# An mLSTM's gate chain in two parts, its selectors in a stage buffer, conditioning steps moved, and latent squares in two sums

## The chip, the cores and the metric

The kernel runs on one core of a Trainium2 chip. The core has five engines with queues of their own that work in order: TensorE (PE, matmuls into PSUM), VectorE (DVE), ScalarE (ACT), GpSimd (POOL) and SyncE (SP, which issues the transfers here). The metric is the device time of one launch in microseconds (us), the median of several runs.

## The reference, cut to what matters

Two layers over 512 latent and 256 context tokens of 1024 channels. Layer 0 mixes tokens with a bidirectional mLSTM, layer 1 with windowed attention; a squared-ReLU MLP follows each, and all are modulated by a conditioning vector.

```python
for i in range(DEPTH):                       # 2 layers
    mod_l = split(silu(c) @ ada_w[i] + ada_b[i], 6);  mod_c = the same with c_ctx
    u = modulate(rms_norm(h, norm_mix[i]), mod_l[0], mod_l[1])       # latent
    uc = modulate(rms_norm(hc, norm_mix[i]), mod_c[0], mod_c[1])     # context
    y, yc = mixer(uc, u)
    h = h + mod_l[2] * y
    h = h + mod_l[5] * sq_relu_mlp(modulate(rms_norm(h, norm_ffn[i]), mod_l[3], mod_l[4]), w1, w2)
    ...                                      # the same for hc
return rms_norm(h, final_norm)

# the mLSTM, per head and direction, in chunks of 128 tokens
q, k, v, o, gates = split(u @ w_in, splits)      # log_i, log_f = gate, log_sigmoid(gate)
b = cumsum(log_f)
m = running maximum of the stabiliser;  w = exp(...), exp(-m)
h = (wq @ v + carry_w * (q @ c0)) / maximum(abs(den), exp(-m))
y = (rms_norm(h) * head_norm * sigmoid(o)) @ w_out
```

## The kernel before

All products are of fp32 data. Each factor is split into a high part and a rest (`whi` and `wlo` of a weight, `uH` and `uL` of the latent activations), and `mm3` (L96 to L98) makes three matmuls of them. Weights come in units of 128 x 1024: SP transfers one to a slot of `raw` (a ring of three slots in this stage), ACT casts it to `whi` (L876), and DVE, or POOL where the caller says so, makes `wlo` (L877). `whi` and `wlo` have four slots each. PSUM is used by two rings, `mm` with three banks and `at` with five. The tokens are treated in two groups, C (256 context columns) and L (512 latent ones).

The conditioning product that isn't needed at the start is spread through the program in steps: `ada_step` (from L249) transfers 512 KB to a slot of the same `raw` ring and multiplies it on DVE in one or two instructions (`adap`, L261). Who calls it decides where they lie: the output gate (`ogate`, by `dense_steps`) at each unit taken, `v_steps` at every second row block, `ada_until` at the MLP's first part.

Layer 0's mixer is `layer0_mix`. It projects q, k and the gates, starts the generator `gates`, runs `v_steps` for the first heads' v (v copied out of PSUM by ACT at L698), then the output gate of the first head pair (`ogate(0)`, copied out at L715), then the rest of the gates, and then `core(p)` for four head pairs p, between whose steps the projections of the next pair are put. `gates` makes a chain of some twenty small instructions on 40 partitions by 768 columns: log-sigmoid on ACT (L613, L614), running sums and maxima as scans on DVE (L619 to L623), three exponentials on ACT (L646, L651, L652), rests on POOL (L625, L642, L648), and then transposes on PE whose results ACT copies to `tok1` and `tok2` (L659, L664). `core` begins with transposes of k (L750), the products `kp` on DVE (L753) and `carry` (L740), a matmul of the gate rows `cst` with the selectors `es`, which POOL writes in `new_es` (L721).

Between the mixer and the MLP, the output projection of the latents (`out_late`) adds to hL; for each of its eight blocks ACT squares the new hL (L290) and the squares are added up into one tile `ssL` (L294), five adds on POOL and then two on DVE. `norm_rc` (L307) sums that over partitions on PE, DVE and POOL make the reciprocal root (L310, L312), and PE spreads it (L320). The MLP's first part, `plain` in `ffn0`, works beside this: four hidden blocks m, first for C (needing no latents), with two hooks after m=0 and m=1 that run the norm, then for L, then `back` multiplies the hidden blocks `h` with the second weight.

The order on each engine is set by a scheduler with a cost model of its own, which may move instructions against the order of the code; `keep_in_program_order` pins one. The line numbers are those of the kernel before; in the kernel after they are one higher in the first hundreds and up to eleven higher from `gates` on (L642 is L653 there, L646 L657, L648 L659, L651 L662, L652 L663, L698 is L709, L740 is L751, L753 is L764, L876 is L887, L877 is L888, L261 is L262).

## Time and profile before

| what | value |
|---|---|
| median of three runs | 1568.58 us (1566.23 to 1571.36) |
| the profiled execution | 1573.33 us, span 1571.5 us |
| PE busy | 1519.8 us, 97% of the span |
| DVE busy | 1123.5 us, 71% |
| ACT busy | 744.2 us, 47% |
| POOL busy | 341.3 us, 22% |

PE has 52 us without work, so most of what a reordering can give lies in its waits and in the stretches after them in which its granted clock is below full. The timeline rows below tell, for each instruction, when it started, how long it or the group took, and in brackets how long its engine had been idle before it and what ended that. SPq rows are the issues of transfers.

### The profile page before, as it was taken

The numbers are of one execution on the slowest core, as the hardware profiler recorded it, in microseconds if no ns is written. First come the engines' busy times: TensorE is split into PE (matmuls) and PEld (weight loads), VectorE is DVE, ScalarE is ACT, GpSimd is POOL, SyncE is SP. The second block draws the span as 40 slices with busy tenths as digits, with TensorE's granted clock in tenths as the row PEclk, the third lists the DMA queues.
The fourth block names the chain that finished last, engine by engine and source line by source line (L and its number), as shares of the span: only waits on it lengthen the run. The fifth ranks groups of instructions, "written<-read, shape, count | busy, mean of one in ns | idle before, by whom it ended". The sixth has DMA issues, their size and how long they took to land.

```text
span 1571.5 us, 23851 instructions
## 1 busy us (share of the span) xinstructions
PE 1519.8 (97%) x9110; PEld 1365.5 (87%) x9110; DVE 1123.5 (71%) x2064; ACT 744.2 (47%) x1506; POOL 341.3 (22%) x333
## 2 busy tenths in 40 slices
PE   7989999999999999999999999899999999999998
PEld 5778888878889999999999999788887888888886
DVE  3666556478777797876776668777888785767687
ACT  4534343334473533424325255566666665545454
POOL 0221111112213222233223322354443100000000
PEclk9989999999999999999999999999999999999999
DMA  8323223234321343343443421011101424150321
GB/s 311 131 74 108 94 95 94 79 101 138 101 68 67 105 136 123 133 148 119 149 135 120 134 81 66 23 41 41 41 28 55 157 82 151 40 170 32 107 68 54
DMA packets 47849, 157.28 MB, mean 100 GB/s; under 512 B 5327, under 2 KB 8911, under 8 KB 47607
## 3 DMA queue, kind: packets, MB, share of 16 engines
q1 hardware_dynamic: 46560, 154.25, 29.4%
q8 instruction: 72, 1.18, 0.3%
q10 hardware_dynamic: 1175, 1.51, 0.3%
q14 instruction: 42, 0.34, 0.1%
HBM read 153.64 MB, written 2.10 MB: 99 GB/s over the span
## 4 chain that ended last, share of the span: by engine, by line
PE 71%; DVE 8%; issue 6%; POOL 5%; ACT 4%; DMA 1%; POOLq 0%; DVEq 0%; ACTq 0%
PE mm L96 16%; PE mm L97 16%; PE mm L98 16%; DVE adap L261 2%; PE p L98 2%; PE p L96 2%; PE p L97 2%; PE pt L1793 1%; PE pj L96 1%; PE pj L98 1%; PE pj L97 1%; DVE wlo L877 1%; PE at L832 1%; ACT whi L876 1%; PE av L1809 1%
## 5 line engine op out<-in xcount | busy, mean ns | idle before, releaser
L877 DVE TENSOR_TENSOR wlo<-raw,whi 128x1024 fp32r<-128x1024 f32 (+2 forms) x152 | 182.6, 1205 | 87.9 <-ACT whi L876 87.1
L876 ACT CAST whi<-raw 128x1024 fp32r<-128x1024 f32 (+2 forms) x155 | 154.0, 1000 | 139.1 <-PE mm L97 74.7
L96 PE MATMUL mm<-uH,whi 128*128 128x512 f32 (+1 forms) x496 | 191.4, 390 | 3.9 <-ACT v L698 3.9
L97 PE MATMUL mm<-uL,whi 128*128 128x512 f32 (+1 forms) x496 | 188.8, 382 | 0.4 <-DVE uL L331 0.4
L98 PE MATMUL mm<-uH,wlo 128*128 128x512 f32 (+1 forms) x496 | 188.9, 382 | 0.0
L261 DVE SCALAR_TENSOR_TENSOR adap<-raw,crow 128x1024 bf16<-128x1024 f32 x128 | 167.0, 1305 | 21.6 <-DMA raw<-ada 20.8
L96 PE MATMUL mm<-h,whi 128*128 128x384 f32 x512 | 173.7, 339 | 4.0 <-DVE hL L1110 2.2
L97 PE MATMUL mm<-h,whi 128*128 128x384 f32 x512 | 172.9, 338 | 0.5 <-DVE h L877 0.5
L98 PE MATMUL mm<-h,wlo 128*128 128x384 f32 x512 | 172.6, 337 | 0.0
L96 PEld LDWEIGHTS mm<-uH,whi 128*128 128x128 f32 x496 | 94.0, 191 | 19.8 <-ACT v L698 4.2
L876 ACT CAST whi<-sum 128x512 fp32r<-128x512 f32 (+1 forms) x42 | 31.8, 760 | 166.3 <-PE mm L97 76.4
L98 PEld LDWEIGHTS mm<-uH,wlo 128*128 128x128 f32 x496 | 94.5, 191 | 17.9 <-issue 0.3
L97 PEld LDWEIGHTS mm<-uL,whi 128*128 128x128 f32 x496 | 94.6, 191 | 17.0 <-issue 1.0
L96 PEld LDWEIGHTS mm<-h,whi 128*128 128x128 f32 x512 | 96.4, 188 | 5.2 <-ACT h L876 2.6
L97 PEld LDWEIGHTS mm<-h,whi 128*128 128x128 f32 x512 | 96.4, 188 | 1.3 <-DVE h L877 1.2
L98 PEld LDWEIGHTS mm<-h,wlo 128*128 128x128 f32 x512 | 96.5, 188 | 0.0
L877 DVE TENSOR_TENSOR wlo<-wb,whi 128x1024 fp32r<-128x1024 f32 x49 | 59.2, 1222 | 35.9 <-ACT whi L876 35.8
L877 DVE TENSOR_TENSOR h<-r,h 128x384 fp32r<-128x384 f32 (+2 forms) x100 | 56.6, 568 | 35.4 <-ACT h L876 35.2
L876 ACT CAST whi<-wb 128x1024 fp32r<-128x1024 f32 x49 | 51.6, 1054 | 60.9 <-PE mm L97 27.1
L98 PE MATMUL p<-t,wlo 128*128 128x384 f32 x224 | 75.4, 337 | 0.3 <-DVE wlo L877 0.3
L97 PE MATMUL p<-t,whi 128*128 128x384 f32 x224 | 75.2, 336 | 0.0
L96 PE MATMUL p<-t,whi 128*128 128x384 f32 x224 | 75.2, 336 | 0.0
(396 smaller groups left out, 4175.2 us busy)
## 6 DMA issues: line engine op xcount, KB each, us to landing
raw<-ada SPq DMA_DIRECT2D x80, 512.0 KB, 3.5
raw<-w SPq DMA_DIRECT2D x64, 512.0 KB, 3.5
raw<-w2a SPq DMA_DIRECT2D x32, 512.0 KB, 3.5
wb<-w2b SPq DMA_DIRECT2D x28, 512.0 KB, 3.6
adaw<-ada SPq DMA_DIRECT2D x16, 512.0 KB, 5.7
hL<-xT SPq DMA_DIRECT2D x16, 256.0 KB, 3.7
raw<-wqk SPq DMA_DIRECT2D x8, 512.0 KB, 4.0
raw<-wv SPq DMA_DIRECT2D x8, 512.0 KB, 3.5
```

What stands on the lines that cost most here:

```text
L96: mm(out=out, lhsT=ah, rhs=bh, start=start, stop=False)
L97: mm(out=out, lhsT=ah, rhs=bl, start=False, stop=False)
L98: mm(out=out, lhsT=al, rhs=bh, start=False, stop=stop)
L261: self.tc.keep_in_program_order(nc.vector.scalar_tensor_tensor(out=pr, in0=w, scalar=0.5, in1=self.crow[:, v, :], op0=ALU.mult, op1=ALU.mu ...
L832: mm(out=o[hh][:, i * VW:(i + 1) * VW], lhsT=pw[g, d, hh][:, i, :], rhs=v[:, 3 * g + i, hh, :], start=False, stop=i == 2)
L876: keep(self.nc.scalar.copy(out=hi, in_=src))
L877: keep((eng or self.nc.vector).tensor_tensor(out=lo, in0=src, in1=hi.bitcast(F32), op=ALU.subtract))
L1793: nc.tensor.transpose(out=pt[:, i * P:(i + 1) * P], in_=ps_[i][:, n * P:(n + 1) * P], identity=self.ident)
L1809: mm(out=o, lhsT=vv, rhs=pl, start=False, stop=n == len(blks) - 1)
```

## The change

1. **Gate chain in two parts.** `gates` yields once more, behind the scans; `layer0_mix` runs it to there before the output gate is begun. The subtraction t1 = li - b (L625) moves from POOL to DVE. The three exponentials are pinned to each other's order.
2. **Selectors.** `es` comes from the pool of the stage (`ml`) instead of the mixer's (`mc`), and the first `new_es` is called before the output gate.
3. **Conditioning steps.** A `dense_steps` call that has POOL make `wlo` (the first output gate) calls no `ada_step`; `v_steps` of later pairs call it at three of six row blocks (j = 4, 5, 0) instead of at j = 1, 3, 5.
4. **Latent squares.** In layer 0's output projection the first four blocks' squares go into a sum L on POOL, the other four into a sum D on DVE, and one more add on DVE (L560 of the kernel after) joins them.
5. **First part of the MLP.** One unit of w1 fewer is fed ahead, the fourth is fed inside the C blocks; the hooks of the norm come after m=1 and in the middle of m=2; the L blocks run in pairs, the first four of their eight channel blocks interleaved, the rest one block after the other.

```diff
@@ -106,7 +106,8 @@
                     w[m] = self.unit(srcs(m), eng)
                 else:
                     w[m] = self.take(eng)
-                    self.ada_step()
+                    if not eng:
+                        self.ada_step()
             hi, lo = w[m]
             n = xs[g](0)[0].shape[-1]
             ps = self.mm.tile([P, 512], F32, name="mm", tag="mm")
@@ -286,7 +287,7 @@
         elif kt:
             sq = self.np.tile([P, n], F32, name="sq", tag=f"sq{n}", bufs=2)
         else:
-            sq = self.np.tile([P, n], F32, name=f"ss{g}", tag=f"ss{n}", bufs=1 if n == 512 else 2)
+            sq = self.np.tile([P, n], F32, name=f"ss{g}", tag=f"ss{n}", bufs=2)
         nc.scalar.activation(out=sq, in_=h, func=AF.Square)
         if apart or kt == 0:
             st.setdefault(g, []).append(sq)
@@ -297,15 +298,15 @@
 
         return self.norm_bc(self.norm_rc(st, g))
 
-    def norm_rc(self, st, g):
+    def norm_rc(self, st, g, keep=lambda i: i):
 
         nc = self.nc
         nb = st[g][0].shape[-1] // P
         ps = self.at.tile([P, 512], F32, name="at", tag="at")
         for j in range(nb):
             for i, acc in enumerate(st[g]):
-                nc.tensor.matmul(out=ps[:, j:j + 1], lhsT=acc[:, j * P:(j + 1) * P], rhs=self.ones, start=i == 0,
-                                 stop=i == len(st[g]) - 1)
+                keep(nc.tensor.matmul(out=ps[:, j:j + 1], lhsT=acc[:, j * P:(j + 1) * P], rhs=self.ones, start=i == 0,
+                                      stop=i == len(st[g]) - 1))
         rs = self.np.tile([P, 4], F32, name="rs", tag="rs", bufs=2)[:, 0:nb]
         nc.vector.tensor_scalar(out=rs, in0=ps[:, 0:nb], scalar1=1.0 / D, scalar2=EPS, op0=ALU.mult, op1=ALU.add)
         rc = self.np.tile([P, 4], F32, name="rc", tag="rc", bufs=2)[:, 0:nb]
@@ -439,10 +440,12 @@
             self.qk_out(qkv, (acc["C"][1:], acc["L"][1:]))
             for _ in self.v_steps(0, qkv[2], rows, wv):
                 pass
+            next(gt)
             self.begun, self.plan = [], [a["wo"][i] for i in range(2)]
             for p in range(1, 4):
                 self.plan += [a[w][2 * p + i] for w in ("wo", "wqk", "wv") for i in range(2)]
             self.plan += [a["wout"][m, :, 0:6 * P] for m in range(6)]
+            self.new_es(0)
             so = self.ogate(0, xs, nc.gpsimd)
             for _ in range(6):
                 next(so)
@@ -451,7 +454,6 @@
             with tc.tile_pool(name="mc", bufs=1, reuse_waits="tile") as mc:
                 self.mc = mc
                 self.late = []
-                self.new_es(0)
                 yu = {}
                 for p in range(4):
                     core = self.core(p, qkv)
@@ -548,7 +550,14 @@
                 for i in range(2):
                     sl = slice((m % 4 * 2 + i) * P, (m % 4 * 2 + i + 1) * P)
                     self.mm3(t, wl[m // 4][0][:, sl], wl[m // 4][1][:, sl], *xs[g](6 + i), new and i == 0, i == 1)
-                self.norm_add(self.st, g, n, self.out_add(m, g, t), nc.vector if n > 5 else None)
+                x = self.out_add(m, g, t)
+                if g == "C":
+                    self.norm_add(self.st, g, n, x, nc.vector if n > 5 else None)
+                else:
+                    self.norm_add(self.st, "DL"[n < 4], n % 4, x, nc.vector if n > 3 else None)
+                    if n == 7:
+                        s0, s1 = self.st["L"][0], self.st["D"][0]
+                        nc.vector.tensor_tensor(out=s0, in0=s0, in1=s1, op=ALU.add)
                 if g == "L" and n < 2:
                     hooks[n]()
             hooks = self.norm_hooks(g)
@@ -564,7 +573,7 @@
             else:
                 self.u0["L"] = self.new_u(cx=False)["L"]
             self.norm_whole(g, int(g == "C"), x[0])
-        return [lambda: x.append(self.norm_rc(st, g)), whole]
+        return [lambda: x.append(self.norm_rc(st, g, self.tc.keep_in_program_order)), whole]
 
     def gates(self, psc, psl):
 
@@ -622,7 +631,9 @@
             scan(m[FW, 0:NL], lf[FW, 0:NL], li[FW, 0:NL], m[FW, T - 1:T], op0=ALU.add, op1=ALU.max)
             scan(m[BW][:, ::-1], lf[BW][:, ::-1], li[BW][:, ::-1], 0.0, op0=ALU.add, op1=ALU.max)
             nc.vector.tensor_tensor(out=aa, in0=b, in1=m, op=ALU.subtract)
-            nc.gpsimd.tensor_tensor(out=t1[R], in0=li, in1=b, op=ALU.subtract)
+            nc.vector.tensor_tensor(out=t1[R], in0=li, in1=b, op=ALU.subtract)
+            yield
+            keep = tc.keep_in_program_order
 
             cp = nc.vector.tensor_copy
             cp(out=ae[FW], in_=aa[FW, P - 1::P])
@@ -643,13 +654,13 @@
 
             az = b
             nc.vector.tensor_tensor(out=ch(az), in0=ch(aa), in1=bc(m0), op=ALU.add)
-            nc.scalar.activation(out=az, in_=az, func=AF.Exp)
+            keep(nc.scalar.activation(out=az, in_=az, func=AF.Exp))
             cp(out=cst[R], in_=az)
             nc.gpsimd.tensor_tensor(out=cst[64:104], in0=az, in1=cst[R].bitcast(F32), op=ALU.subtract)
 
             nc.vector.tensor_tensor(out=ch(aa), in0=ch(t1[R]), in1=bc(ae), op=ALU.add)
-            nc.scalar.activation(out=t1[64:104], in_=aa, func=AF.Exp)
-            nc.scalar.activation(out=t2, in_=m, func=AF.Exp, scale=-1.0)
+            keep(nc.scalar.activation(out=t1[64:104], in_=aa, func=AF.Exp))
+            keep(nc.scalar.activation(out=t2, in_=m, func=AF.Exp, scale=-1.0))
             yield
             for c0, n in ((0, 4), (4, 2)):
                 ps = self.at.tile([P, 512], F32, name="at", tag="at")
@@ -696,7 +707,7 @@
                 if kt == 3:
                     yield
             self.nc.scalar.copy(out=v[:, j, :, 0:128], in_=ps[:, :256].rearrange("p (h e) -> p h e", e=128))
-            if p and j % 2:
+            if p and j in (4, 5, 0):
                 self.ada_step()
             yield
 
@@ -717,7 +728,7 @@
 
     def new_es(self, p):
 
-        self.es = self.mc.tile([104, 2, P], F32R, name="es", tag="es", bufs=2)
+        self.es = self.ml.tile([104, 2, P], F32R, name="es", tag="es", bufs=2)
         self.nc.gpsimd.tensor_copy(out=self.es.rearrange("r d (h e) -> r d h e", e=64),
                                    in_=self.esel.rearrange("r (d c) -> r d c", d=2)[:, :, 2 * p:2 * p + 2].unsqueeze(3)
                                    .broadcast_to([104, 2, 2, 64]))
@@ -1007,32 +1018,55 @@
 
         def plain(hid):
 
-            ws = [self.begun.pop(0) for _ in range(4)]
+            ws = self.begun
+            self.begun = []
             pools = [("mm", self.mm)] * 3 + [("at", self.at)]
-            for g in "CL":
-                xs = self.xs(self.u0)
-                for m in range(4):
-                    hi, lo = ws[m]
-                    n = xs[g](0)[0].shape[-1]
-                    ps = pools[m][1].tile([P, 512], F32, name="mm", tag=pools[m][0])[:, :n]
-                    for kt in range(KT):
+
+            def xs(g, kt):
+                return self.xs(self.u0)[g](kt)
+
+            def begin(g, m):
+                n = xs(g, 0)[0].shape[-1]
+                return pools[m][1].tile([P, 512], F32, name="mm", tag=pools[m][0])[:, :n]
+
+            def part(g, m, ps, half):
+                hi, lo = ws[m]
+                for kt in range(4 * half, 4 * half + 4):
+                    sl = slice(kt * P, (kt + 1) * P)
+                    self.mm3(ps, hi[:, sl], lo[:, sl], *xs(g, kt), kt == 0, kt == KT - 1)
+                if not half:
+                    return
+                r = r_tile(ps.shape[-1])
+                nc.scalar.activation(out=r, in_=ps, func=AF.Relu)
+                nc.scalar.activation(out=r, in_=r, func=AF.Square)
+                if g == "C":
+                    self.split(r, *[x[:, P:H] for x in hid[m][1]])
+                else:
+                    self.split(r[:, 0:H], *hid[m][0])
+                    self.split(r[:, H:NL], *[x[:, 0:P] for x in hid[m][1]])
+            for m in range(4):
+                ps = begin("C", m)
+                part("C", m, ps, 0)
+                if m == 2:
+                    hooks[1]()
+                part("C", m, ps, 1)
+                if m == 1:
+                    hooks[0]()
+                    self.feed(True)
+                    ws.append(self.begun.pop())
+            for i in range(2):
+                pss = [begin("L", 2 * i + m) for m in range(2)]
+                for kt in range(4):
+                    for m in range(2):
+                        hi, lo = ws[2 * i + m]
                         sl = slice(kt * P, (kt + 1) * P)
-                        self.mm3(ps, hi[:, sl], lo[:, sl], *xs[g](kt), kt == 0, kt == KT - 1)
-                    r = r_tile(n)
-                    nc.scalar.activation(out=r, in_=ps, func=AF.Relu)
-                    nc.scalar.activation(out=r, in_=r, func=AF.Square)
-                    if g == "C":
-                        self.split(r, *[x[:, P:H] for x in hid[m][1]])
-                        if m < 2:
-                            hooks[m]()
-                    else:
-                        self.split(r[:, 0:H], *hid[m][0])
-                        self.split(r[:, H:NL], *[x[:, 0:P] for x in hid[m][1]])
-                        self.feed()
-                        if m % 2:
-                            blocks(m // 2)
-                        if m == 1:
-                            self.ada_until(0, 5)
+                        self.mm3(pss[m], hi[:, sl], lo[:, sl], *xs("L", kt), kt == 0, False)
+                for m in range(2):
+                    part("L", 2 * i + m, pss[m], 1)
+                    self.feed()
+                blocks(i)
+                if i == 0:
+                    self.ada_until(0, 5)
 
         def seven(hid, m0, m1):
             banks = [("mm", self.mm), ("at", self.at)] * 3 + [("at", self.at)]
@@ -1117,8 +1151,7 @@
                 self.plan += [f for i in range(2) for f in pair_w1(4 * c + i, 4 * c + 2 + i)]
             self.plan += [unit_w2(c, i) for i in range(4)]
         self.plan += [lambda pr=pr, i=i: self.unit(a["wskv"][pr, i]) for pr in range(2) for i in range(2)]
-        for _ in range(2):
-            self.feed(True)
+        self.feed(True)
         for c in range(NC):
             hid = [[pair(f"h{t}", k) for t in range(2)] for k in range(4)]
             if c == 0:
```

**ACT, the copies of v, the exponentials and what follows before the mixer's heads.** In the names, `whi_999` and `whi_1172` are the third and fourth unit of the output gate's weight wo and `whi_1302` the first of wqk (`whi_993`, `whi_1160`, `whi_1290` after). Before:

```order
L698 COPY v_702<-mm_760 128x2x128
L652 ACT_TABLE_LOAD
L652 ACTIVATE gi_653<-m_655 40x768
L698 COPY v_702<-mm_786 128x2x128
L646 ACTIVATE b_656<-b_656 40x768
L698 COPY v_702<-mm_812 128x2x128
L651 ACTIVATE t1_658<-aa_657 40x768
L876 CAST whi_999<-raw_997 128x1024
L698 COPY v_702<-mm_838 128x2x128
L876 CAST whi_1172<-raw_1170 128x1024
L715 ACTIVATE hL0_907<-mm_882 128x512
```

After:

```order
L709 COPY v_687<-mm_745 128x2x128
L709 COPY v_687<-mm_771 128x2x128
L709 COPY v_687<-mm_797 128x2x128
L887 CAST whi_993<-raw_991 128x1024
L709 COPY v_687<-mm_823 128x2x128
L657 ACT_TABLE_LOAD
L657 ACTIVATE b_656<-b_656 40x768
L662 ACTIVATE t1_658<-aa_657 40x768
L663 ACTIVATE gi_653<-m_655 40x768
L887 CAST whi_1160<-raw_1158 128x1024
L726 ACTIVATE hL0_903<-mm_878 128x512
L887 CAST whi_1290<-raw_1288 128x1024
```

All copies of v and the cast of wo's third unit now stand ahead of the table load, which waits for DVE's L645, and exp(-m), which waited for the scan and stood among the copies, comes last of the three.

**POOL, the same place.** `wlo_1000` is the split of wo's third unit (`wlo_994` after). Before:

```order
L877 TENSOR_TENSOR wlo_867<-raw_864,whi_866 128x1024
L877 TENSOR_TENSOR wlo_873<-raw_870,whi_872 128x1024
L625 TENSOR_TENSOR t1_658<-gi_653,b_656 40x768
L642 TENSOR_TENSOR ast_644<-aa_657,ast_644 40x768
L648 TENSOR_TENSOR cst_645<-b_656,cst_645 40x768
L877 TENSOR_TENSOR wlo_1000<-raw_997,whi_999 128x1024
L721 COPY es_958<-esel_633 104x256
```

After:

```order
L682 MEMSET v_687 128x12
L732 COPY es_864<-esel_633 104x256
L682 MEMSET v_956 128x12
L732 COPY es_1278<-esel_633 104x256
L888 TENSOR_TENSOR wlo_869<-raw_866,whi_868 128x1024
L888 TENSOR_TENSOR wlo_875<-raw_872,whi_874 128x1024
L653 TENSOR_TENSOR ast_644<-aa_657,ast_644 40x768
L888 TENSOR_TENSOR wlo_994<-raw_991,whi_993 128x1024
```

The subtraction L625 is gone from POOL, the split of wo's third unit stands ahead of `cst`, and the first two selectors are written ahead of the splits.

**DVE, the head pair p=2, ahead of kp.** `wlo_2582` is a unit of wo, `wlo_2713` the first of the next wqk (`wlo_2700` after). Before:

```order
L261 SCALAR_TENSOR_TENSOR adap_2537,mod0_81<-raw_2535,crow_625 128x1024
L261 SCALAR_TENSOR_TENSOR adap_2539,mod0_81<-raw_2535,crow_625 128x1024
L877 TENSOR_TENSOR wlo_2582<-raw_2579,whi_2581 128x1024
L267 TENSOR_TENSOR mod0_81<-mod0_81,sm_67 128x16
L261 SCALAR_TENSOR_TENSOR adap_2587,mod0_81<-raw_2585,crow_625 128x1024
L261 SCALAR_TENSOR_TENSOR adap_2589,mod0_81<-raw_2585,crow_625 128x1024
L753 TENSOR_TENSOR kp_2550<-at_2551,tok1_646 128x384 x2
L753 TENSOR_TENSOR kp_2550<-at_2557,tok1_646 128x384 x2
```

After:

```order
L262 SCALAR_TENSOR_TENSOR adap_2447,mod0_81<-raw_2445,crow_625 128x1024
L262 SCALAR_TENSOR_TENSOR adap_2449,mod0_81<-raw_2445,crow_625 128x1024
L262 SCALAR_TENSOR_TENSOR adap_2574,mod0_81<-raw_2572,crow_625 128x1024
L262 SCALAR_TENSOR_TENSOR adap_2576,mod0_81<-raw_2572,crow_625 128x1024
L888 TENSOR_TENSOR wlo_2700<-raw_2697,whi_2699 128x1024
L764 TENSOR_TENSOR kp_2537<-at_2538,tok1_646 128x384 x2
L764 TENSOR_TENSOR kp_2537<-at_2544,tok1_646 128x384 x2
```

A conditioning step and the add of `mod` are gone ahead of kp, and the split of wqk, which came after kp, stands ahead of it.

## Rows read from the trace of the kernel before

**Rows 1.** PE timeline: first instruction after each wait; start, busy, what, [idle before, releaser]

```profile
93.60 0.80 PE L96 MATMUL mm<-uH,whi 128*128 128x512 f32 x1 [3.95 <-ACT v L698]
...
108.89 0.41 PE L740 MATMUL at<-cst,es 104*128 104x384 f32 x1 [1.81 <-issue]
...
264.82 0.42 PE L740 MATMUL at<-cst,es 104*128 104x384 f32 x1 [1.66 <-DVE kp L753]
...
337.65 0.41 PE L740 MATMUL at<-cst,es 104*128 104x384 f32 x1 [1.61 <-DVE kp L753]
...
436.99 0.74 PE L307 MATMUL at<-ones,ssL 128*128 128x1 f32 x5 [1.84 <-DVE ssL L294]
```

**Rows 2.** windows: stretch, PE, PEld, DVE, ACT, POOL busy, granted clock (PEclk), DMA, GB/s

```profile
93.60:99.30 5.70, 5.70 (x13) 4.46 (x14) 1.92 (x3) 3.56 (x6) 4.09 (x3) 0.50 0.00 0
...
110.16:116.80 6.64, 6.64 (x41) 4.44 (x40) 4.38 (x11) 0.70 (x3) 0.40 (x1) 0.77 0.26 81
...
437.00:444.30 7.30, 7.30 (x36) 7.30 (x37) 3.58 (x6) 2.58 (x6) 1.02 (x1) 0.53 0.47 148
```

**Rows 3.** timeline of ACT, 78 to 109 us

```profile
78.34 0.85 ACT L614 ACTIVATE aa<-aa 40x768 f32<-40x768 f32 x1
...
91.15 1.28 ACT L652 ACT_TABLE_LOAD   x1 [9.72 <-DVE m L622]
...
107.07 1.04 ACT L876 CAST whi<-raw 128x1024 fp32r<-128x1024 f32 x1 [4.29 <-DMA raw<-wqk]
```

**Rows 4.** timeline of DVE, 81 to 95 us

```profile
81.26 0.94 DVE L616 SCALAR_TENSOR_TENSOR gz<-gz,aa 40x768 f32<-40x768 f32 x1
...
82.30 1.75 DVE L619 TENSOR_TENSOR_SCAN b<-t,gz 8x768 f32<-8x768 f32 x1
...
86.54 3.23 DVE L623 TENSOR_TENSOR_SCAN m<-gz,gi 8x768 f32<-8x768 f32 x1
...
92.68 0.55 DVE L641 CAST ast<-aa 40x768 fp32r<-40x768 f32 x1
...
93.16 0.94 DVE L645 TENSOR_TENSOR b<-aa,m 40x768 f32<-40x768 f32 x1
```

**Rows 5.** timeline of POOL and of the transfers that SP issues

```profile
85.94 2.22 POOL L625 TENSOR_TENSOR t<-gi,b 40x768 f32<-40x768 f32 x1 [6.95 <-issue]
...
93.38 2.42 POOL L642 TENSOR_TENSOR ast<-aa,ast 40x768 fp32r<-40x768 f32 x1 [5.22 <-DVE ast L641]
...
99.24 2.39 POOL L877 TENSOR_TENSOR wlo<-raw,whi 128x1024 fp32r<-128x1024 f32 x1
...
102.75 0.33 SPq L80 DMA_DIRECT2D raw<-wqk  x1
```

**Rows 6.** timeline at p=2: SP, SP, ACT, DVE, DVE

```profile
257.59 0.33 SPq L258 DMA_DIRECT2D raw<-ada  x1
...
260.13 0.33 SPq L80 DMA_DIRECT2D raw<-wqk  x1
...
263.54 1.05 ACT L876 CAST whi<-raw 128x1024 fp32r<-128x1024 f32 x1 [1.98 <-DMA raw<-wqk]
...
263.65 1.95 DVE L753 TENSOR_TENSOR kp<-at,tok 128x384 f32<-128x384 f32 x4
...
267.37 1.22 DVE L877 TENSOR_TENSOR wlo<-raw,whi 128x1024 fp32r<-128x1024 f32 x1
```

**Rows 7.** timeline of PE, the first latent matmuls of the MLP

```profile
447.69 0.40 PE L96 MATMUL mm<-uH,whi 128*128 128x512 f32 x1
...
448.39 0.40 PE L96 MATMUL mm<-uH,whi 128*128 128x512 f32 x1
```

**Rows 8.** DVE's first adap and PE's first matmuls with h in the MLP

```profile
465.21 1.22 DVE L261 SCALAR_TENSOR_TENSOR adap<-raw,crow 128x1024 bf16<-128x1024 f32 x1
...
469.50 0.33 PE L96 MATMUL mm<-h,whi 128*128 128x384 f32 x1
...
470.02 0.35 PE L96 MATMUL mm<-h,whi 128*128 128x384 f32 x1
```

## The prediction, made before the changed kernel ran

> **What bounds the kernel now.** I read the times first: the profiled execution took 1573.33 us (span 1571.5) and the median of three runs is 1568.58. The profiled one lies 0.3% above that median, so I work out differences on the profiled time axis and take them off the median. TensorE (PE) is busy for nearly all of the span, and then I looked for the few places at which it is not. In layer 0's mixer and behind it there are five that the change touches: 3.95 us at 93.6 until a copy of v, 1.81 at 108.9 with no named releaser, 1.66 at 264.8 and 1.61 at 337.7 until kp, and 1.84 at 437.0 until the sum of squares ssL [rows 1]. Together that is 10.9 us, the most that these waits can give. Next the granted clock: after three of these waits PE runs for a while at the lower of its two levels (1.2 in place of 2.4 GHz), all of 93.6 to 99.3 (granted 0.50), about half of 110.2 to 116.8 (0.77 on average), nearly all of 437.0 to 444.3 (0.53) [rows 2]. So a wait costs more than its length where what follows on PE is what sets the end.
>
> Then why. At 93.6 ACT stands with its queue blocked: after its copies of v it takes the table load for exp(-m) and is idle for 9.72 us until DVE's scan that writes m is done, at about 91.1 [rows 3]; the v copies queued behind it can't free their PSUM banks, and PE runs out of banks at 89.65. At 108.9 the matmul L740 waits for a bank that the copy of tok on ACT frees, and that copy is queued behind the cast of wqk, which began at 107.07 after 4.29 us of waiting for its transfer [rows 3]. The transfer was issued only at 102.75 [rows 5]. So the second wait hangs on a chain that goes from the gates' scans over POOL to a free slot of the raw ring.
>
> **The gate chain.** The change takes away ACT's block: all six v copies and the cast of wo's third unit now precede the table load. PE then runs from 89.65 on without the 3.95 us. Before, it went from 93.60 to its arrival at L740 (108.89 less 1.81, 107.08) in 13.48 us, of which 5.70 at half clock; at full clock that stretch is 2.85 shorter, so it arrives at 89.65 + 13.48 - 2.85 = 100.3. That is not the end, since L740 still waits for the chain, which I follow by rows:
> - The logarithm on ACT ends at 78.34 + 0.85 = 79.19 [rows 3]; DVE's L616 started only at 81.26, behind two adap of a conditioning step [rows 4]. That step is gone from here (-2.07).
> - The subtraction li-b moves from POOL to DVE: +0.95, by the 0.94 of a DVE subtraction of the same shape [rows 4].
> - The scan L623 took 3.23, another scan of 768 columns 1.75 [rows 4]; the only thing beside it was that subtraction on POOL, 85.94 to 88.16 [rows 5]. I take it that the scan is back at 1.75 (-1.48); the other end is 0, if its form is slow by itself.
> - So the cast of ast, which ended at 93.23 [rows 4], ends at 93.23 - 2.07 + 0.95 - 1.48 = 90.6.
> - POOL's ast takes 2.42, and now the split of wo's third unit, 2.39, comes before cst [rows 5]: 90.8 + 2.4 + 2.4 = 95.6. SP's queue has two ada steps fewer ahead of wqk, and the one that remains takes a slot that a split before the gates has freed. So wqk goes out at about 95.65.
> - Cast 4.32 after the issue, as before (102.75 to 107.07), and L740 1.82 after the start of the cast, as before: 101.8. The exps on ACT are over before that: 91.6 + 1.28 (table) + three of about 0.9, and the cast of wo's fourth unit.
>
> L740 at 101.8 in place of 108.89 is **-7.1**; without the faster scan -5.6. PE's wait there stays near 1.5, so I keep the low clock after it. If PE didn't fall to the lower level, 6.64 x 0.23 = 1.5 more would be saved [rows 2]. kp on DVE gets behind two adap and two splits, and starts about 0.5 after L740 as it did about 0.4 after it before; it is no term.
>
> The Trainium skill has a rule on this step (GPSIMD Engine Reference, section 1, Specifications): GpSimd's SBUF interfaces are shared with VectorE, and DVE instructions with two SBUF inputs contend for them. The scan's 3.23 agrees, but DVE's subtraction L645 took 0.94 although POOL's ast began 0.2 us into it, which speaks against it [rows 4, 5]. By the rule the scan must speed up once POOL is quiet, and L740 comes at 101.8; by L645's row the rule is no ground for that, and L740 may come at 103.3 (-5.6).
>
> The es selectors move to a buffer of the stage and their casts to an earlier place on POOL, where POOL is idle. Nothing waited for them: 0.
>
> **Conditioning steps, p = 1 to 3.** Three steps for each v section instead of every second one. At p=1 what precedes kp on DVE is the same: 0. At p=2 the step and the mod before kp go, but the split of wqk comes in their place. Before, the slot freed at 257.59 took an ada and the one freed at 260.13 took wqk, whose cast began 3.41 later [rows 6]. After, wqk gets the slot of 257.59: cast 261.0, 1.05 long, split 1.22, kp at 263.3 instead of 263.65 [rows 6]. But L740 now comes 3 matmuls earlier on PE, and these 3 (0.70, as from 447.69 to 448.39 [rows 7]) follow the wait instead of filling it: -0.4 + 0.7 = **+0.3**. Ends: -0.4, and +2.0 if PE, idle for 2.0 us now, falls to the lower clock (priced like the stretch at 110). At p=3 a seventh adap (1.22) replaces a split of 768 columns (0.95) ahead of the kp that ends PE's wait at 337.65 [rows 1], two matmuls more come before the wait, and the seventh may have to wait for its transfer: between -0.2 and +1.0, **+0.5**, nearer the end with the transfer, since the ring of three slots is full there.
>
> **Squares in two sums.** Before, seven adds run one behind the other into one sum, five on POOL and two on DVE, and the last lets PE go at 436.99 [rows 1]. With two sums POOL adds three and DVE three and the join, in two chains side by side, so that ssL hangs on ACT's last square and no longer on the adds. I put it a little earlier, near 436.7, and PE has 6 matmuls of 256 columns (0.7 us by the 0.23 for 512, halved) more before it. So the wait falls from 1.84 to about 0.8. What it gives is bounded by what follows: the first latent matmul was at 447.69 [rows 7], right behind the last context one. If the lower clock stays away too, that gives 7.3 x 0.47 = 3.4 of which the wait's own 1.0 is a part in my count, since u's chain through the norm limits it: 3.4 at most, 1.0 without the clock. I take **-1.6**, nearer to the lower end, because both waits of 1.8 were followed by the low clock [rows 1, 2]. A cost: one unit of w1 fewer is fed ahead, its cast and split now lie beside the squares; u's chain covers it.
>
> **First part of the MLP.** Three conditioning steps in place of two: 2 adap x 1.22 = 2.44 on DVE, which has much queued there [rows 8]. The latent blocks come in pairs, so the hidden block m=2 is done only 2.8 us before PE wants it, not 5.6. Its split on DVE now stands behind four adap and three sums: 465.2 + 4 x 1.22 + 3 x 0.5 (half of the 0.94 for 768 columns, an estimate) = 471.6, and 0.5 for itself, against 470.7 at which PE asks for it (7 matmuls of 0.17 after 469.50 [rows 8]). That is 1.4, and m=3's split, behind two adap more, may add a little. **+1.5**, between 0 and +3.
>
> Sum: -7.1 + 0.3 + 0.5 - 1.6 + 1.5 = -6.4, and 1568.58 - 6.4 = **1562.2 us**. The rest of the program keeps its order: 0.
>
> **Rivals.**
> 1. The clock stays at its upper level behind both waits: 1.5 at the gates and 1.8 more at the squares, -9.7, **1558.9**. For it: shorter waits. Against: two of the three stretches in [rows 2] follow waits of 1.8.
> 2. What the gates give is paid back by waits later: the low clock at p=2 (+2.0 in place of +0.3), p=3 +1.0, MLP +3, the scan not faster (-5.6), squares -1.0: -0.6, **1568.0**. For it: DVE is the queue that all of these share and it is nearly full. Against: all ends at once.
> 3. Slower: the ring of three raw slots. If at p=2 and p=3 the transfer that kp's queue waits for comes one landing (3.4) late, each also with a stretch of half clock like that of 437 (3.4), that is +13.6 on top of -7.2 for the rest (-7.1 - 1.6 + 1.5): +6.4, **1575.0**. It decides from 3.6 us for each place on. Against: at p=2 the slot is freed 2.5 us earlier than wqk's was.
> 4. The change doesn't shorten the chain: wqk still goes out at 102.75 because POOL's queue is late, the v wait becomes a wait at L740: 0.3 + 0.5 - 1.6 + 1.5 = +0.7, **1569.3**. Against: no step of the chain that I followed gets a later start.
>
> **How the numbers follow.** Forecast 0.50, rival 1 0.17, rival 2 0.20, rival 3 0.06, rival 4 0.07. A measurement of this kernel tells about 0.3% from no change, 4.7 us. The forecast's own range is -8.5 to -4, and a little of it lies within 0.3%; all of rival 1 is faster, rivals 2 and 4 are the same, with a small part of 2 and all of 3 slower: faster 0.62, same 0.30, slower 0.08. The range reaches from the part of rival 1 near 1557 to rival 2 at 1568.0: 1557.0 to 1568.0.
>
> **What would show it.** Right: PE has no wait before the output gate near 90; the exps run after six v copies; wqk issued near 96, L740 near 102 with a wait of 1 to 2 us; the scan of 768 columns near 1.75; the wait for ssL under 1 us; short new waits for h near the first MLP part. Wrong: wqk issued after 99, a wait over 3 us at L740, kp's waits at p=2 or p=3 over 3 us, or a latent matmul that starts as late after the squares as before.

## The result, and the profile after

The changed kernel takes **1556.34 us** (median of 11 runs, 1555.20 to 1566.28), against 1568.58 for the kernel before in the same runs: ratio 0.9935, interval 0.9918 to 0.9951, that is 8 to 13 us less and clear of the 4.7 us of noise. By the ratio, which is the steadier figure, 1568.58 becomes 1558.4, inside the forecast range; the plain median lies 0.7 below its low end. Timed again on another chip (e9), the ratio was 0.9942. The profiled execution has a span of 1554.5 us (1571.5 before) and PE busy for 1509.6 us.

First the list of what PE waited for in the kernel after, 60 to 480 us (total, count, longest):

```profile
PE at L751 <- ACT tok L670: 1.5, 1, 1.5
PE at L751 <- DVE kp L764: 1.1, 1, 1.1
PE mm L96 <- ACT whi L887: 0.3, 1, 0.3
PE at L321 <- POOL rc L313: 0.3, 1, 0.3
PE mm L97 <- DVE uL L489: 0.3, 1, 0.3
...
PE at L308 <- DVE ssL L560: 0.2, 1, 0.2
```

The five waits of [rows 1], 10.9 us together, have become three of 2.8 us together: the one for v and the one for kp at p=2 are gone. Three new ones of 0.3 us each add 1.0. But the two first profiles differ by 17 us in span, and waits alone don't make that. I put the starts of the same matmuls into a table, from the PE timelines of two profiles of each kernel (e7 is the kernel before again, e9 the kernel after again):

| stretch on PE, us | before | before, e7 | after | after, e9 |
|---|---|---|---|---|
| start to the first v matmul | 72.21 | 69.13 | 69.33 | 68.92 |
| to the first matmul with es (L740, L751) | 36.68 | 36.70 | 29.33 | 29.48 |
| to the last of p=3 | 228.76 | 228.62 | 227.62 | 227.54 |
| to the first matmul with h in the MLP | 131.85 | 126.51 | 126.32 | 126.34 |
| to the end | 1102.0 | 1103.5 | 1101.9 | 1101.9 |

The first and the fourth stretch of the first profile of before are chance: the same program does them 3.1 and 5.3 us faster in e7. In the fourth the granted clock is 1.00 behind p=3 and ssL in e7, where it was 0.59 and 0.53 in the first profile. In the first stretch both have 1.00 on record from 20 to 40 us, yet a matmul of 512 columns still takes 0.80 us at 35.44 in the first profile and 0.48 at 35.83 in e7; why is not shown. A third profile of the kernel after, e8, has 29.88, 227.88 and 128.11 in the middle three rows. What repeats is -6.8 to -7.4 in the gates and about -1 over the head pairs.

**The gate stretch.** Timeline of the kernel after: ACT, DVE, POOL, SP's issue, PE.

```profile
88.45 1.28 ACT L657 ACT_TABLE_LOAD   x1 [1.27 <-DVE b L656]
...
96.79 1.05 ACT L887 CAST whi<-raw 128x1024 fp32r<-128x1024 f32 x1 [2.56 <-DMA raw<-wqk]
...
81.42 1.75 DVE L632 TENSOR_TENSOR_SCAN m<-gz,gi 8x768 f32<-8x768 f32 x1
...
90.10 0.95 DVE L661 TENSOR_TENSOR aa<-t,ae 40x768 f32<-40x768 f32 x1 [1.73 <-POOL ast L653]
90.97 2.76 DVE L658 CAST cst<-b 40x768 fp32r<-40x768 f32 x1
...
94.92 2.84 DVE L262 SCALAR_TENSOR_TENSOR adap<-raw,crow 128x1024 bf16<-128x1024 f32 x1
...
87.65 2.42 POOL L653 TENSOR_TENSOR ast<-aa,ast 40x768 fp32r<-40x768 f32 x1 [11.55 <-DVE ast L652]
90.14 3.17 POOL L888 TENSOR_TENSOR wlo<-raw,whi 128x1024 fp32r<-128x1024 f32 x1
93.88 2.80 POOL L659 TENSOR_TENSOR cst<-b,cst 40x768 fp32r<-40x768 f32 x1 [0.56 <-DVE cst L658]
...
93.34 0.33 SPq L80 DMA_DIRECT2D raw<-wqk  x1
...
98.66 0.68 PE L751 MATMUL at<-cst,es 104*128 104x384 f32 x2 [1.48 <-ACT tok L670]
```

ACT's block of 9.72 us at the table load [rows 3] is 1.27. The scan is back at 1.75 from 3.23 [rows 4]. The split of wo's third unit now lies between ast and cst on POOL, and wqk goes out right behind it, at 93.34 instead of 102.75 [rows 5]; its cast follows 3.45 later, and L751 comes 1.87 behind that. Windows of the kernel after, behind the matmuls that were waits (stretch, five busy times, granted clock, DMA share, GB/s); [rows 2] is the same view of before:

```profile
98.66:106.00 7.34, 7.34 (x41) 5.36 (x43) 6.37 (x13) 1.53 (x8) 0.40 (x1) 0.77 0.48 145
252.08:260.00 7.92, 7.73 (x53) 5.41 (x53) 7.14 (x14) 2.02 (x7) 0.00 (x0) 1.00 0.41 133
326.28:334.00 7.72, 7.72 (x61) 5.39 (x61) 7.14 (x16) 1.58 (x6) 0.00 (x0) 1.00 0.42 136
421.84:429.00 7.16, 6.81 (x43) 6.44 (x44) 5.05 (x8) 2.95 (x6) 2.04 (x1) 0.76 0.47 151
```

The lower of the two levels is still granted for a part behind L751 (0.77, as after the 1.81 of before) and around the norm's matmuls (0.76), and no longer for 93.6 to 99.3, where PE now runs.

**p=2**, kernel after: SP's issues, DVE, and L751, which has no wait. Answers to [rows 6].

```profile
230.62 0.33 SPq L259 DMA_DIRECT2D raw<-ada  x1
244.30 0.33 SPq L80 DMA_DIRECT2D raw<-wqk  x1
...
249.78 1.23 DVE L888 TENSOR_TENSOR wlo<-raw,whi 128x1024 fp32r<-128x1024 f32 x1
250.92 1.95 DVE L764 TENSOR_TENSOR kp<-at,tok 128x384 f32<-128x384 f32 x4
...
252.08 0.41 PE L751 MATMUL at<-cst,es 104*128 104x384 f32 x1
```

**Squares and MLP**, kernel after: PE and POOL at the norm, then DVE's and PE's first rows of the MLP's second product, which answer to [rows 8].

```profile
421.16 0.39 PE L96 MATMUL mm<-uC,whi 128*128 128x256 f32 x1 [0.33 <-ACT whi L887]
421.84 1.02 PE L308 MATMUL at<-ones,ssL 128*128 128x1 f32 x8 [0.17 <-DVE ssL L560]
...
423.31 2.04 POOL L313 TENSOR_TENSOR rc<-rs,mhalf 128x4 f32<-128x4 f32 x1 [5.53 <-DVE rs L311]
...
425.42 1.11 PE L321 MATMUL at<-ident,rc 128*128 128x128 f32 x4 [0.33 <-POOL rc L313]
...
447.28 1.22 DVE L262 SCALAR_TENSOR_TENSOR adap<-raw,crow 128x1024 bf16<-128x1024 f32 x1
...
453.26 0.55 DVE L888 TENSOR_TENSOR h<-r,h 128x384 fp32r<-128x384 f32 x1
...
452.60 0.33 PE L96 MATMUL mm<-h,whi 128*128 128x384 f32 x1
```

The wait for ssL is 0.17 instead of 1.84, and h arrives without a wait. But `rc` on POOL takes 2.04 us, twice what it took before; the section on the prediction comes back to this.

### The profile page after: what moved, and what is told of

Read it like the earlier page. It is cut to its first block, busy times and chain, and to the rows that moved or that the text cites. A ratio compares the mean times of both kernels' runs of the same rounds, so it can differ in the third digit from the quotient of the medians.

```text
span 1554.5 us, 23844 instructions
## 1 busy us (share of the span) xinstructions
PE 1509.6 (97%) x9110; PEld 1358.2 (87%) x9110; DVE 1126.9 (72%) x2067; ACT 743.3 (48%) x1506; POOL 341.2 (22%) x330
## 3 DMA queue, kind: packets, MB, share of 16 engines
q8 instruction: 72, 1.18, 0.3%
## 4 chain that ended last, share of the span: by engine, by line
PE 74%; DVE 8%; issue 5%; POOL 5%; ACT 4%; DMA 2%; POOLq 0%; DVEq 0%; ACTq 0%
PE mm L96 16%; PE mm L98 16%; PE mm L97 16%; PE p L98 2%; PE p L97 2%; PE p L96 2%; PE pt L1826 1%; DVE adap L262 1%; PE at L843 1%; ACT whi L887 1%; PE pj L96 1%; PE pj L98 1%; PE pj L97 1%; DVE wlo L888 1%; PE av L1842 1%
## 5 line engine op out<-in xcount | busy, mean ns | idle before, releaser
L97 PE MATMUL p<-t,whi 128*128 128x384 f32 x224 | 75.2, 336 | 0.0
```

Of the source, the lines that this page charges most:

```text
L97: mm(out=out, lhsT=ah, rhs=bl, start=False, stop=False)
```

## The experiments

My theory: the gates' chain gives most of the gain, and its three ingredients (the two parts, the scan, wqk's earlier issue) add up as in the prediction. The rival: the gates' gain is paid back by later waits and the clock, and the whole comes from several small parts.

### The parts alone

Gates, es and the rule for the first output gate alone; then v_steps alone; then the squares and the MLP alone.

```diff
# e1_gate_only, on the kernel before
+                    if not eng:
+                        self.ada_step()
...
+            next(gt)
...
+            self.new_es(0)
...
+            nc.vector.tensor_tensor(out=t1[R], in0=li, in1=b, op=ALU.subtract)
+            yield
# e2_steps_only, on the kernel before
-            if p and j % 2:
+            if p and j in (4, 5, 0):
```

> The kernel before with the gate part alone: gates cut in two, li - b on DVE, exponentials pinned, selectors early, no conditioning step at the first output gate; v's conditioning steps, the squares and the MLP's first part as before. Theory (each wait is worth its length, and the chain to wqk's transfer sets L740): no wait near 90, L740 at 101 to 102 in the profile in place of 108.89, about 7 us saved (ratio 0.9955), and the later waits for kp and ssL stay at 1.6 to 1.8 us. Rival (DVE's queue gives it back at the later waits): the waits for kp grow by the 7 us or so, under 3 us saved.

> The kernel before with only the conditioning steps of v_steps moved (j = 4, 5, 0 in place of 1, 3, 5). Theory from the trace of the changed kernel: the wait for kp at p=2 goes (1.66), the one at p=3 shrinks by about 0.5, and 2 to 5 us are saved, the upper end if the low clock after p=3's wait goes too. Rival (the prediction's term): wqk's split stands before kp and comes late, 0.8 us lost.

> The kernel before with only the squares in two sums and the rewritten first part of the MLP. Theory: the wait for ssL falls from 1.84 to under 0.5 us, no new wait at the first products with h, 2 us saved (1 to 3). Rival (the prediction's term for the MLP): a wait of 1 to 1.5 us at the first products with h takes it back, 0 to 0.5 us saved.

Measured: the gates alone 0.9985 (0.9973 to 0.9996), the steps alone 0.9982 (0.9966 to 0.9998), squares and MLP alone 0.9997 (0.9985 to 1.0008). That is -2.4, -2.8 and -0.5, together -5.7, where the whole gives -9 to -10. The gates, my largest term, seemed worth a third of it. Yet the gates' stretch in e1's profile is the one of the whole change: 29.71 from the first v matmul to the first with es. So the gain is there, and part of it is lost elsewhere. e1's result fits neither text: the later waits stay as the theory said, and the time is the rival's. In e2 the theory holds, without a wait at p=2; the prediction's term for p=2 does not. In e3 the time is the rival's, but no wait at the first products with h takes the gain back; what does is told below. PE's waits in e1, and the window behind the one at p=2:

```profile
PE at L744 <- DVE kp L757: 3.4, 2, 1.8
PE at L744 <- ACT tok L663: 1.9, 1, 1.9
PE at L308 <- DVE ssL L295: 1.8, 1, 1.8
...
253.53:261.70 8.17, 8.17 (x47) 5.51 (x48) 6.14 (x13) 1.64 (x4) 0.00 (x0) 0.79 0.42 128
```

In both profiles of before the clock after the p=2 wait was full; here it is granted at 0.79. I ran the same kernel again to see whether that repeats:

> The kernel before with the gate part alone, profiled and timed again, nothing changed against the first one. Theory (the gate part takes 7.0 us from the first v matmul to L740 every time, and its executions give about 3.5 us of that back in stretches of the lower clock behind the waits that it leaves standing at L740, p=2, p=3 and ssL): 29.7 us within 0.7 from the first v matmul to L740, at least one stretch below 0.95 behind p=2's, p=3's or ssL's wait, mean granted clock over the timed runs 0.988 to 0.990, ratio near 0.9985. Rival (the first timing was off): ratio 0.9955 and mean clock over 0.991.

It gave 0.998 (0.9964 to 0.9995). In the profile the p=2 wait is 1.81 again, and behind it:

```profile
254.20:262.20 8.00, 8.00 (x35) 5.53 (x36) 5.31 (x9) 1.68 (x5) 0.00 (x0) 0.57 0.45 139
```

Everything that e12's theory forecast came about. What the clock costs can be read in two ways. The windows at p=2 hold 1.7 us (8.17 x 0.21) and 3.4 us (8.00 x 0.43), and the stretch from the first matmul with es to the last of p=3 is 230.40 in e1 and 231.79 in e12, 1.6 to 3.2 us longer than in the two profiles of before. For all timed executions, time x (1 - mean granted clock) estimates the time lost to the lower level: 16.6 us before and 17.4 with the gates alone in e1's runs, 17.3 and 17.4 in e12's. The gates' stretch alone should have saved 2.85 of that (5.70 us at 0.50, [rows 2]), so 3.0 to 3.6 us of loss came back elsewhere. These means are rough: single executions lie between 11 and 27 us. In e9, the whole change, the loss is 14.3 against 17.6 on its chip. So the low stretch at p=2 accounts for 1.7 to 3.4 of the 4 us or so that the gates alone lack, and the rest isn't located. That the parts give less than the whole is itself at the edge of the noise: their sum is -5.7 with about 3.6 us either way, the whole -10.2 with 2.6 and -9.1 with 2.7 in e9. Of the later waits, e2 has none at p=2 and 1.2 (and 0.4 for uL) at p=3, and e3 only 0.17 for ssL. That the low stretch at p=2 follows the wait there is shown by the two profiles; why it does so with the gates alone (behind 1.81 us in both profiles) and not in the kernel before (behind 1.65 and 1.66) is not.

### wqk issued before the gates

If L751 hangs on wqk's cast, then issuing wqk before the conditioning step should take the wait away.

```diff
# e4_wqk_early, on the kernel after; e10_wqk_early is the same again
             for _ in gt:
                 pass
+            for eng in (nc.gpsimd, None, None):
+                self.begun.append(self.unit(self.plan.pop(0), eng))
```

> The changed kernel, with the third and fourth unit of wo and the first of wqk requested right behind the gates' code, so that wqk's transfer stands ahead of the conditioning step in SP's queue and takes the slot that a split on POOL frees near 76. Theory (L740's wait hangs on wqk's transfer by way of the cast ahead of the copy of tok): wqk is issued before 80, the wait of 1.48 us at L740 goes, and if the low clock behind it goes with it, 1.5 to 3.2 us are saved against the changed kernel. Rival (cst on POOL or kp on DVE come as late): the wait stays over 1 us with another releaser, no change against the changed kernel.

> The changed kernel unchanged, timed beside the next two on one chip. Theory (its gain is real and the spread comes from the clock): ratio 0.9935 against the kernel before, within 0.002, with single times from 1555 to 1566. Rival (part of the first ratio was a chance of its runs): 0.996 or above, the sum of the three parts timed alone (0.9985, 0.9982, 0.9997).

> The changed kernel with wqk's transfer requested ahead of the conditioning step, again, beside the changed kernel. Theory: no wait at L740 and 2 to 3 us under the changed kernel of this call (ratio lower by 0.0015 to 0.002). Rival (the first difference, 0.9915 to 0.9935, was between chips): equal within 0.0007.

Measured: 0.9915 (0.9895 to 0.9934) for e4; on another chip, side by side, 0.9942 (0.9925 to 0.996) for the kernel after (e9) and 0.991 (0.9894 to 0.9926) for e10. The issue in e4, the window behind the es matmul, and ACT's cast of wqk in e10, now before the copies of tok without a transfer to wait for:

```profile
76.37 0.33 SPq L80 DMA_DIRECT2D raw<-wqk  x1
...
97.26:105.00 7.74, 7.74 (x51) 5.38 (x51) 5.07 (x11) 2.33 (x11) 0.40 (x1) 1.00 0.31 110
...
95.57 1.05 ACT L889 CAST whi<-raw 128x1024 fp32r<-128x1024 f32 x1 [0.29 <-issue]
```

PE has no wait there in either run and the clock stays at 1.00. From the first v matmul to the first with es it is 27.7 and 28.0 (29.3 to 29.9 after), and from there to the next pair's k 78.0 and 78.3 (79.5). These two stretches give 2.6 us of difference between e9 and e10, as the theory had it; the mean times differ by 4.3, with about 3.4 either way. The estimated loss to the lower level falls from 14.3 to 8.8 us (e9, e10). So the wait of 1.5 that I kept in the forecast, and the low clock behind it, hang on wqk's issue, and this version is faster than both kernels.

```diff
# e11_steps_432, on e10
-            if p and j in (4, 5, 0):
+            if p and j in (4, 5, 0, 1)[:5 - p]:
```

> The kernel with wqk requested early, and four, three and two conditioning steps in v's sections of p=1, 2 and 3 in place of three each: one step moved from the section ahead of p=3's kp, where PE waits 1.16 us, to p=1, where DVE was idle for 8.2 us ahead of kp. Theory: the wait at p=3 falls to 0 to 0.6 us, and 0.5 to 1 us are saved against the kernel with wqk early. Rival (kp's splits of u, which go before it, or a transfer hold it): the wait stays at 1.1 us or more and the time is the same.

0.9911 (0.9895 to 0.9927), no different from e10. One step fewer before the p=3 kp didn't shorten its wait: 1.36, against 1.14 and 0.31 for uL in e10. DVE does four splits of uL ahead of kp where it did three, which is the rival's reading.

### The scan and the two parts

```diff
# e5_sub_on_pool, on the kernel after
-            nc.vector.tensor_tensor(out=t1[R], in0=li, in1=b, op=ALU.subtract)
+            nc.gpsimd.tensor_tensor(out=t1[R], in0=li, in1=b, op=ALU.subtract)
# e6_one_part, on the kernel after
-            next(gt)
...
-            yield
```

> The changed kernel with the subtraction li - b back on POOL, in the gate chain before it. Theory (POOL's two-input instruction slows DVE's scan beside it): the scan of 768 columns that took 1.75 us in the changed kernel takes about 3.2 again, and the cast of ast, which ends 11.3 us after the start of the chain on DVE in the changed kernel, ends 0.5 later (+1.48 - 0.92). Rival (the scan was slow by its form, or by a chance of that profile): the scan stays at 1.75 and the cast of ast ends 0.9 earlier.

> The changed kernel with the gates in one part again (no yield behind the scans), all else as changed. Theory: the table load and the first exponential stand ahead of the last three copies of v again, and PE waits for a copy of v before the output gate; since the chain itself starts as early as in the changed kernel, L740 moves by less than 2 us and most of the gain at L740 (7.3 from the first v matmul to L740) stays. Rival (the split carries the gain): L740 comes 4 us or more later, counted from the first v matmul.

> The kernel before, profiled again, nothing changed. Theory (whether the lower clock follows a wait of 1.6 to 1.8 us differs from one execution to the next): the waits keep their lengths within 0.3 us, but the stretch from the third kp to the first product with h, 135.7 us in the first profile, is 2 to 4 us shorter or the same, and the first v matmul comes anywhere from 68 to 73 us. Rival (the lower clock belongs to the program): all stretches repeat within 0.5 us.

> The changed kernel, profiled again, nothing changed. Theory (as for the kernel before): waits within 0.3 us of the first profile, with stretches of the lower clock in other places or none behind L740 and ssL, and the start up to the first v matmul different by 1 to 4 us. Rival: all stretches repeat within 0.5 us.

One execution each: 1557.79, 1559.15, 1566.29 and 1561.05 us. In e5, POOL's subtraction, the scan that starts inside it, and the es matmul:

```profile
82.28 2.22 POOL L634 TENSOR_TENSOR t<-gi,b 40x768 f32<-40x768 f32 x1 [5.41 <-issue]
...
82.89 3.23 DVE L632 TENSOR_TENSOR_SCAN m<-gz,gi 8x768 f32<-8x768 f32 x1
...
100.79 0.98 PE L751 MATMUL at<-cst,es 104*128 104x384 f32 x2 [2.84 <-ACT tok L670]
```

The scan takes 3.23 again. The move to DVE is worth 0.8 to 1.35 from the first v matmul to es (30.68 against 29.33 to 29.88), a little above the 0.5 that its terms give (1.48 - 0.95).

In e6, with the gates in one part but without the conditioning step: ACT's table load and the first copy of v behind it, POOL's cst, the split of wo, then wqk's issue and cast, and the es matmul.

```profile
87.95 1.28 ACT L655 ACT_TABLE_LOAD   x1 [7.23 <-DVE b L654]
...
90.00 0.35 ACT L707 COPY v<-mm 128x256 f32<-128x256 f32 x1
...
91.11 1.85 POOL L657 TENSOR_TENSOR cst<-b,cst 40x768 fp32r<-40x768 f32 x1 [1.53 <-DVE cst L656]
93.39 2.38 POOL L886 TENSOR_TENSOR wlo<-raw,whi 128x1024 fp32r<-128x1024 f32 x1 [0.42 <-POOL cst L657]
...
95.80 0.33 SPq L80 DMA_DIRECT2D raw<-wqk  x1
...
99.28 1.04 ACT L885 CAST whi<-raw 128x1024 fp32r<-128x1024 f32 x1 [4.32 <-DMA raw<-wqk]
...
101.14 0.98 PE L749 MATMUL at<-cst,es 104*128 104x384 f32 x2 [4.66 <-ACT tok L668]
```

The stretch is 32.51 here, 2.6 to 3.2 more than after and 4.2 less than before. So the two parts are worth some 3 us, and the rest of the gate part about 4: the conditioning step taken out of the chain, the subtraction (0.8 to 1.35 by e5), the pinned exponentials and the early selectors, which no run separates further. The v wait, which I gave to the two parts, was gone in e6 too, although ACT stands idle for 7.23 us at its table load there and comes to the next copy of v no earlier: 21.4 us behind the first v matmul, against 21.0 in before (93.20). The difference is that four copies of v stand ahead of the table load in e6 and three in before, so that PE has one more bank to go on with. The order of the exponentials, which e6 keeps pinned, goes with that: before, it was exp(-m) that stood behind the third copy. What PE then waits for is L749, 4.66 us: there the v wait has in part become a wait for the chain, as rival 4 had it. What the two parts do is let the cast of wo's third unit pass ahead of the exponentials, and with it POOL's split and wqk's issue (24.0 behind the first v matmul after, 27.2 here). Neither text's number fitted (below 2, or 4 and more), and the theory's wait for v didn't come.

e7 put 7.0 us of difference between two profiles of one program: its waits are those of before within 0.05 us, but for L740's (2.37, not 1.81) and a new one of 0.37 for rc, and the clock behind p=3 and ssL is full in e7, where it was 0.59 (first line, of before) and 0.53 [rows 2]:

```profile
337.65:346.00 8.35, 8.35 (x44) 5.22 (x44) 5.29 (x12) 2.41 (x7) 0.00 (x0) 0.59 0.42 152
...
334.45:343.00 8.55, 8.55 (x66) 5.87 (x67) 7.64 (x17) 2.62 (x9) 0.00 (x0) 1.00 0.40 138
424.00:433.00 9.00, 7.18 (x61) 7.01 (x60) 6.47 (x9) 6.42 (x12) 4.78 (x4) 1.00 0.00 1
```

e8, the kernel after again, has the wait at L751 at 2.0, 29.88 for the gates, and the clock at 0.63 in the 8 us behind the norm's first matmul, for 128.11 in the fourth stretch. So waits don't all repeat within the 0.3 us that both theories named, and the first v matmul of e8 came only 0.35 later than in the first profile of after. The rivals, all stretches the same within 0.5, fail in both.

## Why the prediction came out as it did

The direction was right and the sum somewhat small: -6.4 forecast, -10.2 measured (-9.1 in e9). Point by point, with equal clocks compared:

- **Gates, -7.1: measured -7.2 to -7.4 (-6.8 in e8).** The steps held: no v wait, scan 1.75, L751's wait 1.48 (put at 1.5), the low clock kept behind it. wqk went out at 93.34, 24.0 behind the first v matmul; the 95.65 of the forecast is 23.4 behind it on its own axis, so it was 0.6 late. Inside it two errors cancel: the split of wo took 3.17 and not 2.39, the cast came 3.45 after the issue and not 4.32. That the two parts end the v wait was too narrow a reason, as e6 shows, but its end was right.
- **p=2, +0.3: measured -1.5.** This step failed. I gave wqk the slot that an ada had before; it got one a pair of adap earlier still, which wo's second unit had taken before (at 254.56): that unit now went out at 223.95 and the ada at 230.62. wqk's split ended before kp was due, kp started 1.2 ahead of the matmul that had waited for it, and no wait was left to trade for the three matmuls.
- **p=3, +0.5: measured +0.4**, from the pair's first k to that matmul 4.24 against 3.84; the waits in it are 1.15 for kp and a new 0.32 for uL. The clock behind it is no effect: low in one profile of before, full in e7, e1 and after.
- **Squares, -1.6: measured -0.1.** The wait for ssL went even further down than I put it (0.17), but the gain didn't follow. From the first context matmul to the first latent one it is 15.44 in e7 and 15.30 in e3, both at full clock. With the new hooks only 10 matmuls stand between the sums and `rc` where 21 stood, and POOL's 2.04 for `rc` isn't covered: 1.08 of wait in e3 and e10. But `rc` used to take 1.02. Here are POOL's `rc` in before, and the split of w1's fourth unit on DVE in the kernel after, which began 0.05 ahead of `rc` there:

```profile
440.76 1.02 POOL L312 TENSOR_TENSOR rc<-rs,mhalf 128x4 f32<-128x4 f32 x1 [5.44 <-DVE rs L310]
...
423.26 1.23 DVE L888 TENSOR_TENSOR wlo<-raw,whi 128x1024 fp32r<-128x1024 f32 x1
```

In all nine profiles with the new squares and MLP part this split starts 0.05 to 0.06 ahead of `rc`, and `rc` takes 2.04; in all five without, it takes 1.02. The 1.02 more is what the split still had to do, 1.18, less 0.16: the rule told below under "The rule that I weighed wrongly". An estimate from these rows: without that meeting the wait of 1.08 would be near 0, and the squares would have given about 1.1. A third of a us more is lost on the cast of w1's third unit (0.33). So the unit that is fed later, which I had written off as covered by u's chain, costs nearly all that the two sums gain.
- **MLP, +1.5: measured 0.** The adap started 5.3 us ahead of the first h matmul and not 4.3, and the split of m=2 began 453.26, done at 453.81, just when PE came to it (452.60 + 7 x 0.17 = 453.8).

Together -7.3 - 1.5 + 0.4 - 0.1 = -8.5, against -9.1 and -10.2; the rest lies within the intervals (-6.3 to -11.8, and -7.7 to -12.9). That the sum came nearer than its terms is partly luck: the 1.5 that the squares didn't give and the 1.5 that the MLP didn't cost cancel. Rival 1 (the clock stays up) came nearest in time, 1558.9, but its mechanism didn't happen: the low clock after L751 is there in after, e8 and e9. At the gates it did happen in e4 and e10, where the wait was removed; behind the squares the clock is 1.00 in e10 and 0.79 in e4. The first item of rival 2, the low clock at p=2, is what the gates alone run into (e1, e12); with the steps moved it isn't there. Rivals 3 and 4 are refuted for the whole change by the rows at p=2 and by wqk's issue.

**The rule that I weighed wrongly.** The scan's 3.23 is no even slowing. In before, POOL's subtraction ends at 85.94 + 2.22 = 88.16 [rows 5], the scan that began inside it at 86.54 + 3.23 = 89.77 [rows 4]: 1.61 behind, its own 1.75 less 0.14. The same sum fits in the kernel after: the cast at 90.97 (0.55 alone, by [rows 4]) ends 0.42 after POOL's split, adap (1.22 alone) ends 1.08 after cst. It works in both directions: POOL's split began 0.04 after L661 and took 3.17 in place of 2.39, the 0.91 that L661 still had, less 0.13. So whoever starts second waits until the first is done, and its row shows the wait as busy time. Of the 41 adap and wlo of 128x1024 in the kernel after that start inside a sum, subtraction or product on POOL, 38 end within 0.05 of what this gives (POOL's end + 1.22 - 0.14) and 40 within 0.1. The seven that start inside one of POOL's small powers (128x3) keep their 1.22 to 1.23, so not every instruction of POOL holds DVE back; the other way round the powers do wait, as `rc` shows. I had held L645's 0.94 against contention because ast began 0.2 into it; but L645 came first, and it was ast that waited: 2.42, the 1.85 that cst of the same shape takes in e6, and the 0.72 that L645 still had, less 0.15. The Trainium skill says this (SBUF — State Buffer, Who interferes with whom): of a DVE instruction with two SBUF inputs or in a two-port mode, which a cast can be in, and a GpSimd instruction that reads SBUF, the first to issue has the shared ports for its whole length and the other fully blocks. The traces agree, with the numbers above, but for the seven rows inside the powers. Had I read it so, the forecast would have kept the -7.1 with more reason, and seen that the split moved between ast and cst would meet the cast of cst there, and that a split of w1 next to the norm can hold up `rc`.

## What to carry to other kernels

A queue blocked by one early instruction is found by its long idle entry in the timeline, and splitting the work around it pays by what comes forward behind it, here a transfer, more than by the wait that one sees. When a wait is shortened, count the work that lies between it and the next link of its chain: the squares' wait went to `rc`, ten matmuls on. Look there too for work that was moved next to it: a row of POOL or DVE that takes twice its usual time beside one of the other is a wait that no list of waits shows. Where the main engine's clock falls behind some waits and not behind others, parts of a change need not add up, and one profile of each kernel doesn't tell a difference of a few us: compare waits, and the mean clock over several executions.

## What the runs showed that I had not expected

- The lower clock behind a wait is not a fixed cost. Behind the es matmul's wait it was granted each time, in all eleven profiles that have the wait (1.48 to 4.66 us; 0.74 to 0.79 over the 7.5 us behind it), and in none of the three without (e4, e10, e11: 1.00). The granted clock behind p=3's 1.6 was 0.59 in before and 1.00 in e7, e1, e12 and e3; behind p=2's 1.7 it was 1.00 in before, e7 and e3, but behind 1.8 it was 0.79 and 0.57 in e1 and e12; behind ssL's 1.8 it was 0.53 in before, 0.79 in e1, e2 and e12, and 1.00 in e7. What decides stays open.
- It fell with hardly a wait too: 0.76 in the window from 421.84 of the kernel after, whose waits are 0.17 to 0.33; e10 has 1.00 there with waits of 0.17 to 1.08.
- A DVE cast of 0.55 became 2.76, and an adap of 1.22 became 2.84, only by starting inside an instruction of POOL; POOL's `rc` of 1.02 became 2.04 by starting 0.05 behind a split on DVE.
